# Issuing the weight-sum transfers of an output projection some steps sooner, and after the last heads' merges on GpSimd

## The chip, the cores and the metric

The kernel runs on one core of one Trainium2 chip. The metric is the time of one execution on the device in microseconds (us); lower is better. The engines are TensorE (PE; its weight loads are listed as PEld), VectorE (DVE), ScalarE (ACT), GpSimd (POOL) and SyncE (SP). Each takes its instructions in a fixed order, and a transfer (DMA) is an instruction in the order of the engine that issues it.

## The reference, cut to what matters

One layer of a transformer-like block over 512 tokens of width 1024, in fp32: a gated linear attention and a latent attention with 8 heads, merged by gates, then an output projection, then a feed-forward layer.

```python
n = rmsnorm(h, g_mix[l])
proj = n @ w_in[l]
...
y_gla = gla_branch(gq, gk, gv, gr, z_gf, z_gb, ...)
y_mla = mla_branch(cq, ckv, kr, positions, ...)          # softmax attention, 8 heads
merged = jax.nn.sigmoid(z_ma) * y_gla + jax.nn.sigmoid(z_mb) * y_mla
h = h + merged @ w_out[l]                                # 512x1024 times 1024x1024
m = rmsnorm(h, g_mlp[l])
h = h + jnp.square(jax.nn.relu(m @ w_ff1[l])) @ w_ff2[l]
...
return rmsnorm(h, g_final)
```

## The kernel before

Every matmul operand is split into a high and a low part (`split`: ACT copies to the high part, then DVE or POOL subtracts to get the low part, lines 93 and 94), and each product is three matmuls (`mm3`, lines 88 to 90).

**The attention loop.** It runs `n` from 0 to 37. Step `n` does the scores and the exponential of one head and one quarter of the tokens (`att_scores`, `s`, `e`, lines 1017 and 1022), normalises earlier ones (line 1029), transposes (`att_flip`, `tp`, `pT`, line 1037), and every second step multiplies with the values (`att_values`, `av`). When a head is finished, `merge` scales its output on DVE (`tb`, line 1065) and adds the other branch on POOL (`mx`, `my`, line 1068). Heads 2p and 2p+1 fill the two column halves of one pair of tiles, `mx` and `my` of pair p. The last head, 7, merges in two halves: `mx` when its first 256 tokens are ready, `my` with the others. `LAG_C` is 6, so the values of head 6 come at n = 31 and 33, and those of head 7 at n = 35 and 37.

**The projection** multiplies by seven products of half-size blocks instead of eight (products 1, 2, 5, 6, 3, 7, 4, in this order). Its left operands are made pair by pair: `gao` from `mx` (`split_first`, products 1 and 2; its first 256 columns belong to the pair's even head and to product 1, the others to the odd head and product 2), and the sums `yo` and `zo` (`merged_sums`, lines 938 to 941) with their splits `ghyo`, `glyo`, `ghzo`, `glzo` (`split_sum`, products 5, 6, 7, 3). For pair 3 these sums are made after the loop on DVE (`ghbo`, `glbo`, `ghco`, `glco`).

Its right operands are blocks B11, B12, B21, B22 of `w_out`, and sums of them:

- Products 1 and 2 take B11 and B21 as they are (`streamed`, tiles `bo10`, `bo11`, `bo20`, `bo21`; 11 and 13, 21 and 23 are their steps).
- The tiles `w_00`, `w_01` hold block B11, to which `load_onto(B11, B12)` adds B12 (product 5). `w_20`, `w_21` are loaded with B22, then B11 is added, then B12 (product 6), and later B21 (product 4). `w_10`, `w_11` hold B12, to which B22 is added (product 7); `w_30`, `w_31` hold B22 (product 3).
- A plain load (`load_w2`, line 903) is four 256 KB transfers issued by SP. An adding transfer (`load_onto`, line 909) is two 512 KB transfers issued by POOL with an accumulating write, and each waits until what was written to that tile before has landed:

```python
for g, d in enumerate(block_tiles(dst)):
    ...
    nc.gpsimd.dma_start(d, rows.rearrange(...)[:, x // 2], accum_op=ALU.add)
```

After the loop the code of the projection fixes the order of PE, ACT and DVE by hand (`in_program_order(begun, PE_ONLY + SPLITTERS)`), and the order of POOL from the start of the attention loop on is the order of the program text (`in_program_order(attending, (...Pool,))`). In the attention itself a list scheduler orders PE, ACT, DVE and SP. The first four column blocks of the feed-forward weights are `f00f` to `f03f` (line 223), loaded by SP into a ring of three staging buffers that `bo20f` and `bo21f` use too. `goes_behind(late, early, engines)` puts the first instruction of one group behind the last of another on an engine.

Of the kernel before, what the change touches and what calls it, by code (L numbers as in the profile page):

```python
# [56 lines left out]
def tile_block(ctx: ExitStack, tc: tile.TileContext, t, out: bass.AP):  # L57
    nc = tc.nc
# [48 lines left out]
    def traced():  # L107
        return len(nc.cur_bb.bb.instructions)

    def in_program_order(start, engines=None):  # L110

        prev = {}
        for ins in nc.cur_bb.bb.instructions[start:]:
# [4 lines left out]
                issued_after(ins, before)  # L118
            prev[ins.engine] = ins.name

    PE_ONLY = (mybir.EngineType.PE,)
    SPLITTERS = (mybir.EngineType.Activation, mybir.EngineType.DVE)

    def goes_behind(late, early, engines):

        ins = nc.cur_bb.bb.instructions
        for e in engines:
            a, b = [[i for i in ins[x:y] if i.engine == e] for x, y in (early, late)]
            if a and b:
                issued_after(b[0], a[-1].name)  # L130
# [115 lines left out]
    def proj_run(begun, src, half=None, ks=range(KD)):  # L246
        wh, wl, acc = begun
        c = slice(0, S) if half is None else slice(half * 256, half * 256 + 256)
        for k in ks:
            mm3(acc[:, c], wh[:, k, :], wl[:, k, :], src[k][:, 0, c], src[k][:, 1, c], k == 0, k == KD - 1)  # L250
        return acc
# [620 lines left out]
    def split_sum(left, src, m_lo, m_hi, name, rest=nc.vector):  # L872
        h, l = u2(f"gh{name}", F32R), u2(f"gl{name}", F32R)
        split(h, l, src, rest)
        left[m_lo] = h[:, 0:HT], l[:, 0:HT]
        left[m_hi] = h[:, HT:S], l[:, HT:S]
# [22 lines left out]
    def load_w2(qd, x, w=w2, block=None):  # L899

        for g, dst in enumerate(block_tiles(x)):
            for pp_ in range(2):
                nc.sync.dma_start(dst[:, pp_, :], block_rows(w, qd, x if block is None else block, g, pp_))

    def load_onto(dst, x, w):

        for g, d in enumerate(block_tiles(dst)):
            rows = w[4 * g * P : 4 * (g + 1) * P, (x % 2) * S : (x % 2 + 1) * S]
            nc.gpsimd.dma_start(d, rows.rearrange("(k t p) w -> p t k w", t=2, p=P)[:, x // 2], accum_op=ALU.add)  # L909
# [24 lines left out]
    def merged_sums(p, eng):  # L934
        px, qx = merged[p]
        a11, a12, a21, a22 = px[:, 0:HT], px[:, HT:S], qx[:, 0:HT], qx[:, HT:S]
        y, z = u2(f"yo{p}"), u2(f"zo{p}")
        eng.tensor_tensor(y[:, 0:HT], a21, a22, op=ALU.subtract)
        eng.tensor_tensor(y[:, HT:S], y[:, 0:HT], a11, op=ALU.subtract)
        eng.tensor_tensor(z[:, 0:HT], a11, a21, op=ALU.subtract)  # L940
        eng.tensor_tensor(z[:, HT:S], a12, y[:, HT:S], op=ALU.add)
        return y, z
# [99 lines left out]
    def att_values(head, half):  # L1042
        if half == 0:
            avs[head] = ps("mm", f"av{head}")
        acc = avs[head]
        hi, lo = pTs.pop((head, half))
        _, _, vs, c = heads[head]
        for k in range(NT):
            vt = vs[k // 2]
            mm3(acc[:, half * 256 : (half + 1) * 256], vt[:, 0, k % 2, c], vt[:, 1, k % 2, c],  # L1050
                hi[:, k, :], lo[:, k, :], k == 0, k == NT - 1)
        if head < MH - 1:
            if half == 1:
                merge(head, acc, (0, 1))
        else:
            merge(head, acc, (half,))
# [51 lines left out]
    for n, (a, m) in enumerate(steps[:-4]):  # L1108
        ahead = steps[n + 2]
        if a == 0:  # L1110
            for x in {3: (0,), 7: (2, 1), 4: (3,)}.get(m, ()):
                sevens[1].load(x)
        if steps[n + 1] in fillers:
            at = traced()
            begun[steps[n + 1]] = fillers[steps[n + 1]][0]()
            goes_behind((at, traced()), loading, (mybir.EngineType.SP,))
        if n == 1:
            split_sums(x_y, 5, 6)
        if n == 2:
            split_sums(x_z, 7, 3)  # L1120
        if (a, m) == (0, 5):
            load_gates()
            pos_i = u2("pos_i", I32)
            nc.gpsimd.dma_start(pos_i, t["positions"][0].partition_broadcast(P))
        if (a, m) == (0, 4):
            z_chunk_finish(z_acc)
            split_gates()
        if (a, m) in fillers:
            sevens[a].product(m)
            sevens[ahead[0]].prepare(ahead[1])  # L1130
            rest = fillers[a, m][1](begun.pop((a, m)))
            if (a, m) == (0, 6):
                z_acc = rest
        elif m == 7:
            sevens[a].multiply(m)
            sevens[ahead[0]].prepare(ahead[1])
            sevens[a].sinks(m)
        else:
            sevens[ahead[0]].prepare(ahead[1])
            sevens[a].product(m)  # L1140
# [114 lines left out]
    units = up_units(1)  # L1255
    next(units)
    attending = traced()
    sums_of, flipping = {}, {}
    for n in range(4 * MH + LAG_C):
        if n % 2 == 0 and 2 <= n <= 4 * MH:  # L1260
            att_normalise((n - 2) // 4, (n - 2) % 4)
        scored = traced()
        if n < 4 * MH:
            att_scores(n // 4, n % 4)
            if n - 2 in flipping:
                goes_behind((scored, traced()), flipping[n - 2], SPLITTERS)
        scored = scored, traced()
        if 2 <= n % 8 < 7:
            next(units, None)
        if n in (6, 14):  # L1270
            units = up_units(n // 8 + 2)
            next(units)
        b = n - LAG_B
        if 0 <= b < 4 * MH:
            flips = traced()
            att_flip(b // 4, b % 4)
            flipping[n] = flips, traced()
            if b == 0:
                gla_turn(GH - 1, (flips, traced()))

        extra = traced()
        for x, at in (("y", (18, 26, 32)), ("z", (20, 28, 33))):
            if n in at:
                p = at.index(n)
                to = (5, 6) if x == "y" else (7, 3)
                split_sum(wo_left[p], sums_of[p, x], *to, f"{x}o{p}", nc.gpsimd)
        if n in (19, 30):
            p = (19, 30).index(n)
            split_first(wo_left[p], merged[p][0], f"o{p}", nc.gpsimd)
        if n < 4 * MH:  # L1290
            goes_behind((extra, traced()), scored, SPLITTERS[:1])
        if n == 35:
            split_first(wo_left[2], merged[2][0], "o2")
        if n in (11, 13):
            streamed(1, B11, (n - 11) // 2)
        if n in (21, 23):
            streamed(2, B21, (n - 21) // 2)
        if n == 22:
            load_w2(0, B11, w_out)
        if n == 23:  # L1300
            load_w2(0, B21, w_out, B22)
        if n == 25:
            load_onto(B11, B12, w_out)
        if n == 27:
            load_onto(B21, B11, w_out)
        if n == 28:
            load_w2(0, B12, w_out)
            load_w2(0, B22, w_out)
        if n == 31:
            load_onto(B21, B12, w_out)  # L1310
        if n == 34:
            load_onto(B12, B22, w_out)
        c = n - LAG_C
        if c >= 0 and c % 2 == 1:
            att_values(c // 4, (c % 4) // 2)
        if c > 0 and c % 8 == 7 and c // 8 < NP - 1:
            sums_of[c // 8, "y"], sums_of[c // 8, "z"] = merged_sums(c // 8, nc.gpsimd)

    hrow = []
    for i in range(NT):  # L1320
# [12 lines left out]
    def first_half_square(i, c):  # L1333
        hparts[i] = sm(f"hp{i}", 4)
        ms_rows[i] = u4(f"ms{i}", F32, (P, D))
        square_half(hrow[i], c, hparts[i], ms_rows[i], True)

    span = {}

    def second_half_square(i, c):  # L1340
        square_half(hrow[i], c, hparts[i], ms_rows[i], False)
# [43 lines left out]
    def hidden(qd, j):  # L1385

        if qd == 0 and j < 2:
            acc = early[j][2]
        elif qd == 0 and j in (2, 3):
            at = traced()  # L1390
            begun = proj_begin(w1, j * P, f"f{qd}{j}")
            goes_behind((at, traced()), span["norm", NT - 1] if j == 2 else span["evacuate", 1], SPLITTERS)
            acc = proj_run(begun, mT)
        else:
            acc = proj_run(proj_begin(w1, (qd * FQ + j) * P, f"f{qd}{j}"), mT)
        a = u2(f"fa{qd}{j}")
        nc.scalar.activation(a, acc, AF.Relu)  # L1397
        return a
# [154 lines left out]
    fm.evacuate(0, range(4, KD))  # L1553
    first_half_square(3, 1)
    span["evacuate", 0] = at, traced()
    early = [proj_begin(w1, 0, "f00", "mm")]
    wo_product(4, (0,))
    add_rows(2, 0, xs_[0])
    second_half_square(2, 0)
    early.append(proj_begin(w1, P, "f01", "mm"))  # L1560
    wo_product(4, (1,))
    at = traced()
    add_rows(3, 0, xs_[1])
# [90 lines left out]
```

## Time and profile before

| | |
|---|---|
| median of 3 runs | 775.52 us (775.02 to 776.52) |
| the profiled execution's own time | 775.01 us |
| its span, first to last instruction | 773.3 us |
| PE, PEld busy | 757.3 us (98%), 638.1 us (83%) |
| DVE, ACT, POOL busy | 579.7 us (75%), 453.4 us (59%), 152.0 us (20%) |
| TensorE clock granted, mean | 0.997 |
| chain that ended last | PE 87%, DVE 3%, ACT 3%, POOL 2%, DMA 2%, issue 2% |

"Busy" counts the time in which at least one instruction of the engine runs; on PE the instructions overlap, so that the time between two starts (0.23 us for a 128x512 matmul, 0.12 for 128x256) says more than a duration. The attention loop lies at about 305 to 389 us, the projection at 384 to 434, and the feed-forward layer follows to the end.

### The profile page before, as it was taken

How to read it: one execution, taken by the hardware profiler on the slowest of the kernel's cores; microseconds unless marked ns; L12 is line 12 of the kernel's file. 1: busy time of each engine (PE TensorE's matmuls, PEld its weight loads, DVE VectorE, ACT ScalarE, POOL GpSimd, SP SyncE). 2: the span in 40 equal slices, each digit the busy share in tenths (PEclk: the TensorE clock that was granted, in tenths of full speed). 3: DMA queues.
4: the chain of work that ended last, by engine and by line, in shares of the span. 5: the costliest groups of instructions: out<-in, count | busy, mean ns of one | idle time of the engine just before them, and what ended most of it. 6: DMA issues, size and time to landing. Idle time of an engine off the chain costs nothing.

```text
span 773.3 us, 10231 instructions
## 1 busy us (share of the span) xinstructions
PE 757.3 (98%) x3744; PEld 638.1 (83%) x3744; DVE 579.7 (75%) x848; ACT 453.4 (59%) x768; POOL 152.0 (20%) x228
## 2 busy tenths in 40 slices
PE   9999999999999999999979999999999999999996
PEld 7888788889888889898958788888888888888885
DVE  7789999666677766999947776965787578848695
ACT  8456567565466555888825675444644465336644
POOL 0720006160623114045852000000000000000014
PEclk9999999999999999999999999999999999999999
DMA  9733201121324324114997331263115510560002
GB/s 311 248 110 119 79 27 29 55 83 45 90 58 119 51 58 126 44 48 140 282 250 194 109 109 55 68 201 112 55 36 182 158 34 28 174 181 0 28 1 109
DMA packets 97185, 81.28 MB, mean 105 GB/s; under 512 B 15504, under 2 KB 74896, under 8 KB 97136
## 3 DMA queue, kind: packets, MB, share of 16 engines
q1 hardware_dynamic: 93904, 74.33, 31.9%
q0 software_dynamic: 2944, 6.03, 4.2%
q8 instruction: 29, 0.48, 0.3%
q10 hardware_dynamic: 288, 0.28, 0.1%
q14 instruction: 20, 0.16, 0.1%
HBM read 76.96 MB, written 2.10 MB: 102 GB/s over the span
## 4 chain that ended last, share of the span: by engine, by line
PE 87%; DVE 3%; ACT 3%; POOL 2%; DMA 2%; issue 2%; POOLq 0%; SPq 0%; DVEq 0%; ACTq 0%
PE f L89 7%; PE f L90 7%; PE f L88 7%; PE gx L88 4%; PE gx L89 4%; PE gx L90 4%; PE first L326 3%; PE za L88 2%; PE za L89 2%; PE gz L88 2%; PE za L90 2%; PE gz L89 2%; PE gz L90 2%; DMA w<-in_w_out 2%; PE zb L88 1%
## 5 line engine op out<-in xcount | busy, mean ns | idle before, releaser
L1593 POOL DMA_DIRECT2D gfin<-in_g_final x1 | 0.6, 625 | 283.0 <-PE f L90 283.0
L913 DVE TENSOR_TENSOR w<-w,w 128x1024 f32<-128x1024 f32 x32 | 38.7, 1221 | 0.3
L474 POOL COPY v3f<-rrf 128x4 f32<-128x4 f32 x4 | 2.8, 709 | 135.9 <-DVE rrf L457 135.9
L1022 ACT ACTIVATE e<-s,top 128x512 f32<-128x512 f32 x32 | 21.9, 686 | 6.8 <-DVE top L1017 6.5
L1329 DVE TENSOR_TENSOR h<-h,gx 128x512 f32<-128x512 f32 x32 | 21.5, 682 | 1.9 <-PE gx L90 1.8
L94 DVE TENSOR_TENSOR pT<-tp,pT 128x512 fp32r<-128x512 f32 x32 | 21.7, 682 | 1.6 <-ACT pT L93 1.4
L1017 DVE TENSOR_REDUCE top<-s 128x1 f32<-128x512 f32 x32 | 21.6, 679 | 0.9 <-PE s L90 0.7
L1037 PE MATMUL tp<-ident,e 128*128 128x128 f32 x128 | 19.4, 275 | 0.8 <-ACT e L1028 0.8
L93 ACT ACTIVATE pT<-tp 128x512 fp32r<-128x512 f32 x32 | 18.9, 596 | 1.3 <-PE tp L1037 1.0
L88 PE MATMUL av<-pT,v 128*128 128x256 f32 x64 | 19.0, 296 | 0.0
L89 PE MATMUL av<-pT,v 128*128 128x256 f32 x64 | 18.5, 289 | 0.0
L1397 ACT ACTIVATE fa<-f 128x512 f32<-128x512 f32 x32 | 18.5, 578 | 0.0
L93 ACT ACTIVATE ghb<-y 128x512 fp32r<-128x512 f32 x16 | 10.1, 632 | 14.0 <-DVE y L859 14.0
L90 PE MATMUL av<-pT,v 128*128 128x256 f32 x64 | 18.0, 282 | 0.0
L94 DVE TENSOR_TENSOR sc<-sc,sc 128x512 fp32r<-128x512 f32 x16 | 10.9, 691 | 9.5 <-ACT sc L93 9.5
L1037 PEld LDWEIGHTS tp<-ident,e 128*128 128x128 f32 x128 | 14.9, 141 | 3.7 <-ACT e L1028 1.5
L93 ACT ACTIVATE sc<-sc 128x512 fp32r<-128x512 f32 x16 | 9.3, 596 | 11.5 <-DVE sc L545 11.5
L909 POOL DMA_DIRECT2D w<-in_w_out x10 | 12.7, 1454 | 13.5 <-DVE bo60l L94 6.7
L93 ACT ACTIVATE b_00h<-w 128x1024 fp32r<-128x1024 f32 x7 | 7.4, 1059 | 12.3 <-PE gz L90 6.0
L93 ACT ACTIVATE b_20h<-w 128x1024 fp32r<-128x1024 f32 x7 | 7.4, 1061 | 12.1 <-PE gz L90 6.0
L93 ACT ACTIVATE b_10h<-w 128x1024 fp32r<-128x1024 f32 x7 | 7.4, 1061 | 12.1 <-PE gx L90 6.0
L88 PE MATMUL s<-kbuf,q 96*128 96x512 f32 x32 | 14.3, 447 | 0.1
(1665 smaller groups left out, 2939.1 us busy)
## 6 DMA issues: line engine op xcount, KB each, us to landing
w<-in_w_ff SPq DMA_DIRECT2D x64, 256.0 KB, 3.4
w<-in_w_out POOLq DMA_DIRECT2D x10, 512.0 KB, 10.3
grw<-in_w_in SPq DMA_DIRECT2D x8, 512.0 KB, 9.3
gvw<-in_w_in SPq DMA_DIRECT2D x8, 512.0 KB, 4.6
w<-in_w_out SPq DMA_DIRECT2D x16, 256.0 KB, 5.8
x<-in_xt SPq DMA_DIRECT2D x8, 256.0 KB, 5.1
vw<-in_w_first SPq DMA_DIRECT2D x8, 256.0 KB, 5.3
h<-in_x SPq DMA_DIRECT2D x4, 512.0 KB, 16.3
```

Source lines behind the costliest of these rows:

```text
L88: nc.tensor.matmul(acc, lh, rh, start=start, stop=False, skip_group_check=onto)
L89: nc.tensor.matmul(acc, lh, rl, start=False, stop=False, skip_group_check=onto)
L90: nc.tensor.matmul(acc, ll, rh, start=False, stop=stop, skip_group_check=onto)
L93: nc.scalar.activation(hi, src, AF.Copy)
L94: rest.tensor_tensor(lo, src, raw(hi), op=ALU.subtract)
L326: nc.tensor.matmul(f_accs[i], a[:, i * P : (i + 1) * P], b, start=k == 0 and x == 0, stop=k == KD - 1 and x == 2)
L913: nc.vector.tensor_tensor(wq[dst][g], wq[x][g], wq[y][g], op=op)
L1017: nc.vector.tensor_reduce(top, acc, axis=AX.X, op=ALU.max, negate=True)
L1022: nc.scalar.activation(e, acc, AF.Exp, bias=top, accum_out=tot[:, qt % 2 : qt % 2 + 1])
L1037: nc.tensor.transpose(tp[:, k * P : (k + 1) * P], e[:, k * P : (k + 1) * P], ident)
L1329: nc.vector.tensor_tensor(hc, hc, acc, op=op)
L1397: nc.scalar.activation(a, acc, AF.Relu)
```

## The change

The adding transfers and the plain loads in front of them move to earlier steps; the second addition onto B21 moves behind the merges of head 6, and that onto B12 behind those of head 7. The low halves of the sums of pair 2 go from POOL to DVE and some steps later. Four loads of feed-forward columns get an order on SP: none goes ahead of the loads of step 17.

```diff
+    SP_ONLY = (mybir.EngineType.SP,)
...
-    sums_of, flipping = {}, {}
+    sums_of, flipping, span = {}, {}, {}
...
+        if n == 20:
+            load_onto(B11, B12, w_out)
         extra = traced()
-        for x, at in (("y", (18, 26, 32)), ("z", (20, 28, 33))):
+        for x, at in (("y", (18, 26, 34)), ("z", (20, 28, 36))):
             if n in at:
                 p = at.index(n)
                 to = (5, 6) if x == "y" else (7, 3)
-                split_sum(wo_left[p], sums_of[p, x], *to, f"{x}o{p}", nc.gpsimd)
+                split_sum(wo_left[p], sums_of[p, x], *to, f"{x}o{p}", nc.gpsimd if p < 2 else nc.vector)
...
-        if n == 22:
+        if n == 15:
             load_w2(0, B11, w_out)
+        if n == 17:
+            at = traced()
+            load_w2(0, B21, w_out, B22)
+            span["sums"] = at, traced()
         if n == 23:
-            load_w2(0, B21, w_out, B22)
-        if n == 25:
-            load_onto(B11, B12, w_out)
-        if n == 27:
             load_onto(B21, B11, w_out)
-        if n == 28:
+        if n == 24:
             load_w2(0, B12, w_out)
             load_w2(0, B22, w_out)
-        if n == 31:
-            load_onto(B21, B12, w_out)
-        if n == 34:
-            load_onto(B12, B22, w_out)
         c = n - LAG_C
         if c >= 0 and c % 2 == 1:
             att_values(c // 4, (c % 4) // 2)
+        if n == 33:
+            load_onto(B21, B12, w_out)
         if c > 0 and c % 8 == 7 and c // 8 < NP - 1:
             sums_of[c // 8, "y"], sums_of[c // 8, "z"] = merged_sums(c // 8, nc.gpsimd)
+    load_onto(B12, B22, w_out)
...
             begun = proj_begin(w1, j * P, f"f{qd}{j}")            # f02, f03
             goes_behind((at, traced()), span["norm", NT - 1] if j == 2 else span["evacuate", 1], SPLITTERS)
+            goes_behind((at, traced()), span["sums"], SP_ONLY)
...
+    at = traced()
     early = [proj_begin(w1, 0, "f00", "mm")]
+    goes_behind((at, traced()), span["sums"], SP_ONLY)
...
+    at = traced()
     early.append(proj_begin(w1, P, "f01", "mm"))
+    goes_behind((at, traced()), span["sums"], SP_ONLY)
```

In the built program this gives these orders around the change. POOL: `glyo` and `gao` of pair 0, the two adds onto `w_00`, `w_01`; `glzo` of pair 0, the merges of head 3, the sums of pair 1, the two first adds onto `w_20`, `w_21`; the merges of head 4, `glyo` and `glzo` of pair 1, the merges of head 5, the sums of pair 2, `gao` of pair 1, the merges of head 6; then the two second adds onto `w_20`, `w_21`; the merges of head 7; the two adds onto `w_10`, `w_11`. SP: the loads of `w_00`, `w_01`, `w_20`, `w_21`, then `bo21f`, `f00f`, `f01f`, `f02f`, then those of `w_10`, `w_11`, `w_30`, `w_31`. DVE: `glyo` of pair 2 ahead of its `gao`, `glzo` of pair 2 between the two scalings `tb` of head 7. The scheduler's order on PE, ACT and DVE changes by a few places between heads 4 and 7, with the same instructions.

More of the change, by code (lines that the diff above doesn't have):

```diff
@@ L1115, in tile_block @@
             begun[steps[n + 1]] = fillers[steps[n + 1]][0]()
-            goes_behind((at, traced()), loading, (mybir.EngineType.SP,))
+            goes_behind((at, traced()), loading, SP_ONLY)
         if n == 1:
@@ L1336, in first_half_square @@
         square_half(hrow[i], c, hparts[i], ms_rows[i], True)
-    span = {}
     def second_half_square(i, c):
```

## The prediction

> **What bounds the kernel now.** PE is busy for 98% of the span, so I first asked what PE waits for. The list of waits, PE alone, from 383 to 447 us:
>
> ```profile
> PE wox L88 <- ACT gao L93: 5.3, 1, 5.3
> PE f L90 <- DVE f01l L94: 0.4, 1, 0.4
> ```
>
> One wait is 5.3 us; the others are below half a microsecond. Busy time by stretches (the columns are the engines' busy time and counts, then the granted clock, the DMA share and GB/s) shows what follows it:
>
> ```profile
> 390.60:396.10 5.50, 0.17 (x1) 0.00 (x0) 0.01 (x1) 0.46 (x2) 4.88 (x6) 0.98 1.09 296
> 396.10:399.60 3.50, 3.50 (x9) 2.55 (x10) 2.09 (x2) 1.02 (x2) 3.50 (x5) 0.54 1.09 193
> 399.60:404.00 4.40, 4.40 (x21) 3.64 (x20) 3.69 (x7) 2.83 (x4) 0.53 (x1) 1.00 0.90 185
> ```
>
> PE stands still, then runs 3.5 us at a clock of 0.54, then at 1.00. The timeline of PE gives the length exactly:
>
> ```profile
> 390.39 0.39 PE L90 MATMUL wox<-bo11h,gao 128*128 128x512 f32 x1
> ...
> 396.11 0.79 PE L88 MATMUL wox<-bo11h,gao 128*128 128x512 f32 x1 [5.33 <-ACT gao L93]
> ...
> 399.57 0.40 PE L90 MATMUL wow<-bo20h,gao 128*128 128x512 f32 x1
> ```
>
> It waits for `gao` of pair 3, which ACT makes from `mx` of head 6. The timeline of DVE has that head's scaling early, and the timeline of POOL says why `mx` is late:
>
> ```profile
> 382.96 0.67 DVE L1065 SCALAR_TENSOR_TENSOR tb<-tb,av 128x512 f32<-128x512 f32 x1
> ```
>
> ```profile
> 367.88 2.54 POOL L909 DMA_DIRECT2D w<-in_w_out  x2
> ...
> 374.44 2.45 POOL L909 DMA_DIRECT2D w<-in_w_out  x2
> ...
> 383.00 1.29 POOL L94 TENSOR_TENSOR gao<-mx,gao 128x512 fp32r<-128x512 f32 x1
> 386.52 1.20 POOL L909 DMA_DIRECT2D w<-in_w_out  x1 [2.23 <-DMA w<-in_w_out]
> 391.22 1.20 POOL L909 DMA_DIRECT2D w<-in_w_out  x1 [3.50 <-DMA w<-in_w_out]
> 391.97 1.75 POOL L94 TENSOR_TENSOR glyo<-yo,ghyo 128x512 fp32r<-128x512 f32 x1
> 393.20 1.73 POOL L94 TENSOR_TENSOR glzo<-zo,ghzo 128x512 fp32r<-128x512 f32 x1
> 394.42 1.19 POOL L1068 TENSOR_TENSOR mx<-tb,za 128x256 f32<-128x256 f32 x1
> ```
>
> `tb` of head 6 is done at 383.6, but `mx` stands behind the second adds onto `w_20` and `w_21`. Each waits for the first add to its tile (issued from 374.44 on) to land, and behind them come the splits of pair 2's sums. ACT makes `gao` at 395.64, PE starts at 396.11.
>
> **What the stall costs.** PE would have started at 390.39 + 0.23 = 390.62, so it is 5.49 us late. The next eight matmuls take 399.57 - 396.11 = 3.46 us instead of 8 x 0.2275 = 1.82 (21 starts from 399.81 to 404.58), so the low clock costs 1.64 more. Together 7.13 us, if nothing else takes the place of the wait.
>
> **Merges of head 6 ahead of the second adds.** POOL's work up to `gao` of pair 1 keeps its pace: the first adds onto `w_20`, `w_21` take the place at 367.9 that those onto `w_00` had, and the merges, sums and splits behind wait for DVE and ACT as before. `gao` ends at 384.3, `mx` and `my` of head 6 (0.73 and 0.92) at 385.0 and 385.9. ACT is free for `gao` of pair 3 at about 385.4 (its last pieces in this place end at 385.5 now), done 385.8. DVE makes the low half behind `tb` of head 7's second half (388.52 + 0.42), so at about 389.4. PE needs it at 390.62: the wait goes, with 1.2 us to spare.
>
> **The two splits moved to DVE.** Two 128x512 subtractions at 0.69 us (the row of `gao` there has 693 ns) are 1.4 us more on DVE between 385 and 389. DVE now waits 1.88 us for PE ahead of the scaling at 388.52, which covers them. POOL loses 2 x 1.29 us.
>
> **Head 7's merges behind the second adds.** The first adds are issued at 367.9 and 369.1 and landed at most 15.7 us after issue (the list of transfers has this for the one issued at about 377, the slowest), so by 384.8. The second adds then start without a wait at 385.9 and 387.1, and `mx`, `my` of head 7 run from 388.3 to 389.9 (`tb` is ready at 386.6 and 388.9). ACT has `bo50h` ahead, which waits for PE's last use of `bo10` (389.4) and takes 1.04; `gao`'s second half ends at 390.9, its low half behind `bo50l` (1.22 + 0.50) at 392.1. PE needs it for the last pair of product 2, at 390.62 + (6 + 18) x 0.2275 = 396.1. Slack 4 us.
>
> **The sums of blocks.** The second adds land 10.4 us (the issue at 386.5 now) after 385.9 and 387.1: 396.3 and 397.5. ACT splits from there (1.06), DVE 1.22 later behind the additions of product 1 and 2: about 398.6 and 401. Product 6 starts at 390.62 + 54 x 0.2275 = 402.9 and wants `bo61` at 405.6. At the slowest 15.7 they land at 401.6 and 402.8, `bo60` is split at 403.9 and `bo61` at about 406: under 1 us of stall, and perhaps 1 us more through DVE, which is busy from 402.9 to 418 now. I take 0: of the 3 MB that SP issued from 365.6 to 373, ahead of these transfers, the 1 MB for `w_20`, `w_21` is gone by then, and the first adds run 6.5 us sooner. The add onto `w_10` goes out at 389.9 instead of 395.8 for a split now at 413.0.
>
> **SP and the loads moved.** Eight transfers of 256 KB (four took 1.95 us of SP) now stand ahead of `bo21f`, `f00f`, `f01f`. The last four wait for head 2's values, whose scaling begins at 347.65, so `bo21f` goes out at about 350 instead of 346.6 and lands 2.9 us later; ACT takes it at 361.5 now. `f00f` to `f02f` went out at 348.8 to 365.2 for splits at 432 to 441. Cost 0, cover 8 us or more. `w_00` and `w_20` land (5.8 us, the page's median) by 356, before POOL's adds want them.
>
> **The reordered attention.** DVE takes `bo20l` (1.21) and a few others some places earlier. Now PE is busy 40.0 of 40.0 us from 320 to 360 and its waits for `e` at 310.7 and 362.5 are 0.25 and 0.51. From below -0.8 (these go), from above +1.75 (the longest single DVE row there, `bo21l`, in full); I take 0, by the 40.0 row.
>
> **The tail of the projection** (DVE, ACT, POOL and PE in turns, 418 to 444) starts from PE's product 3 and moves with it. Nothing in it depends on an absolute time: the third adds onto `w_20` go out behind `bo60l` as now and land in 6 to 7.2 us for a split 15 us later.
>
> **Sum.** 775.01 - 7.13 = 767.9 for an execution like the profiled one, which lies 0.5 under the median: 768.4.
>
> **The rivals.**
> *A part of the wait comes back* (`bo60` late by the slowest landing, or PE waits in the attention): against it speak the slacks above, for it that DVE has no idle time in the projection. The slowest landing costs 2, the attention 1.75: up to 772.1. A short stall keeps the clock: the idle times of 0.5 us left it at 1.00. The Trainium skill (TensorE: Matmul & The Clock Gate, "HAM oscillation") puts the limit at an idle time of about 3.4 us; the trace has nothing between 0.5 and 5.5. By that rule a new stall of 4 us costs 4 + 1.64: 774.0.
>
> *The change doesn't do what it says*: another instruction on POOL, ACT or DVE holds `gao` back as long as before, 775.5. The order of the built program speaks against it.
>
> *Slower: POOL blocks at the second adds with head 7's merges behind.* They are still in one queue, and now `my` of head 7 and all sums of pair 3 come after them. PE is where it was before when `gao`'s second low half comes 5.5 us after 396.1, at 401.6; `mx` 1.7 us earlier (0.73 + 0.42 + 0.50), the issue of `w_21` (1.20) before it: a first add that lands at 398.7, 29.6 us after its issue. Beyond, each us costs one: 34 us would give 780. For it speaks that POOL waited 2.23 and 3.50 us at this place and that the DMA share was over 1; against it, 15.7 us as the slowest of all.
>
> **How the numbers follow.** 0.2% (1.55 us) is about what a measurement of this kernel can tell from no change. The full gain 0.74, with its own range 767.3 to 770.2 (-0.8 and +1.75 of the attention, some 0.3 of spread); a part of it 0.13, 770 to 774; no change 0.05; slower 0.08, by the blocked queue or an attention that loses over 8 us. Faster by over 0.2% is 0.74 + 0.13 = 0.87. The range leaves out the slower and unchanged cases and the upper third of the partial one: 766.8 to 772.5.
>
> **What would show it.** PE's wait of 5.33 at `wox` gone, its clock 1.00 from 385 to 430; `mx` of head 6 at about 384.3 ahead of L909; no DMA wait on POOL there; product 2 at about 392.0, the first `mb` at 416.5 instead of 423.6. It is wrong if PE waits over 1 us at `wow` or product 6, or if the first `wox` of the projection starts later than 383.6 by over 1 us.

## The result and the profile after

The changed kernel takes 768.11 us (median of 4 runs, 768.01 to 768.70) where the kernel before takes 776.02 (775.02 to 776.63): a ratio of 0.9901 with a 95% interval of 0.9884 to 0.9918. In a second comparison it is 768.36 against 776.37 us, 0.9897 [0.9884, 0.9910]. The profiled executions are 768.70 us (span 767.0) and 767.94 us (span 766.2).

The list of PE's waits from 383 to 447 us in the profile after (total, times, longest) has three lines:

```profile
PE f L90 <- DVE f01l L94: 0.4, 1, 0.4
PE wox L88 <- DVE h L1331: 0.3, 1, 0.3
PE f L89 <- DVE mT L98: 0.3, 1, 0.3
```

The wait of 5.3 us for `gao` is gone and no other has come in this stretch. The three stretches that stood at a clock of 0.98, 0.54 and 1.00 before (columns as there):

```profile
390.60:396.10 5.50, 5.50 (x26) 4.56 (x25) 4.32 (x9) 2.99 (x5) 3.00 (x3) 1.00 1.12 203
396.10:399.60 3.50, 3.50 (x17) 2.92 (x16) 3.50 (x6) 1.85 (x3) 0.26 (x1) 1.00 1.05 225
399.60:404.00 4.40, 4.40 (x21) 3.62 (x21) 4.01 (x6) 2.74 (x7) 3.02 (x4) 1.00 1.10 259
```

PE is busy through all of them at 1.00. The timeline of GpSimd shows the new order (start, length):

```profile
383.85 1.28 POOL L94 TENSOR_TENSOR gao<-mx,gao 128x512 fp32r<-128x512 f32 x1
385.09 0.73 POOL L1069 TENSOR_TENSOR mx<-tb,za 128x256 f32<-128x256 f32 x1
385.79 0.73 POOL L1069 TENSOR_TENSOR my<-tb,za 128x256 f32<-128x256 f32 x1
386.48 2.41 POOL L910 DMA_DIRECT2D w<-in_w_out  x2
388.10 1.55 POOL L1069 TENSOR_TENSOR mx<-tb,za 128x256 f32<-128x256 f32 x1
390.36 0.86 POOL L1069 TENSOR_TENSOR my<-tb,za 128x256 f32<-128x256 f32 x1 [0.71 <-DVE tb L1066]
```

`mx` and `my` of head 6 follow `gao` of pair 1 at once, and the two second adds (L910) start without a wait for a transfer. On VectorE the moved splits are the first and the third line here:

```profile
386.20 0.88 DVE L94 TENSOR_TENSOR glyo<-yo,ghyo 128x512 fp32r<-128x512 f32 x1
387.00 0.68 DVE L94 TENSOR_TENSOR gao<-mx,gao 128x512 fp32r<-128x512 f32 x1
...
387.93 0.68 DVE L94 TENSOR_TENSOR glzo<-zo,ghzo 128x512 fp32r<-128x512 f32 x1
389.86 0.42 DVE L1066 SCALAR_TENSOR_TENSOR tb<-tb,av 128x256 f32<-128x256 f32 x1 [1.25 <-PE av L90]
```

VectorE still waits 1.25 us for PE behind them (1.88 before), so they are covered. Where PE stands is read from its timeline:

```profile
384.60 0.39 PE L88 MATMUL wox<-bo10h,gao 128*128 128x512 f32 x1
...
392.86 0.39 PE L88 MATMUL wow<-bo20h,gao 128*128 128x512 f32 x1
...
417.35 1.04 PE L199 MATMUL mb<-ident,ms 128*128 128x128 f32 x8
```

These three marks and the first `uq` after 286 us (the up-projection of queries, just ahead of the attention) cut every profile of this study into four pieces. The place of that `uq` lies between 291.8 and 293.0 us from run to run, with equal code ahead of it; the pieces behind it repeat within 0.15 us for equal kernels, so parts are weighed by them:

| us | uq to wox (attention) | wox to wow | wow to mb | mb to the end | sum |
|---|---|---|---|---|---|
| before, both profiles | 90.89, 90.91 | 15.30, 15.45 | 24.72, 24.65 | 349.68, 349.63 | 480.6 |
| after, both profiles | 92.00, 92.01 | 8.26, 8.30 | 24.49, 24.49 | 349.65, 349.57 | 474.4 |
| difference | +1.10 | -7.10 | -0.20 | 0 | -6.2 |

The stall gave back 7.1 us, and the attention took 1.1 of it.

### The profile page after: what moved, and what is told of

Its sections match the earlier page's. It is cut to its first block, busy times and chain, and to the rows that moved or that the text cites. A ratio compares the mean times of both kernels' runs of the same rounds, so it can differ in the third digit from the quotient of the medians.

```text
span 767.0 us, 10229 instructions
## 1 busy us (share of the span) xinstructions
PE 755.7 (99%) x3744; PEld 637.4 (83%) x3744; DVE 579.7 (76%) x850; ACT 453.5 (59%) x768; POOL 149.6 (20%) x226
## 4 chain that ended last, share of the span: by engine, by line
PE 91%; DVE 4%; ACT 3%; issue 1%; POOL 0%; DMA 0%; POOLq 0%; SPq 0%; ACTq 0%; DVEq 0%
PE f L89 7%; PE f L90 7%; PE f L88 7%; PE gx L88 4%; PE gx L90 4%; PE gx L89 4%; PE first L327 3%; PE za L88 2%; PE za L89 2%; PE gz L88 2%; PE za L90 2%; PE gz L89 2%; PE gz L90 2%; PE zb L88 1%; PE zb L90 1%; PE zb L89 1%
## 5 line engine op out<-in xcount | busy, mean ns | idle before, releaser
L88 PE MATMUL av<-pT,v 128*128 128x256 f32 x64 | 19.1, 298 | 0.4 <-ACT pT L93 0.4
L88 PE MATMUL s<-kbuf,q 96*128 96x512 f32 x32 | 14.3, 446 | 0.4 <-DVE pT L94 0.4
L1407 ACT ACTIVATE px<-fa 128x256 f32<-128x256 f32 x32 | 13.4, 418 | 1.0
```

Source lines behind the costliest of these rows:

```text
L88: nc.tensor.matmul(acc, lh, rh, start=start, stop=False, skip_group_check=onto)
```

## The experiments

The edit has three parts: the **order** on GpSimd (second adds and the adds onto `w_10` behind the merges), the **transfers** (loads and first adds some steps sooner, with the order on SP), and the **splits** of pair 2's sums on VectorE. Each was run alone, and each was left out.

**The order alone.** The kernel before, with

```diff
-        if n == 31:
-            load_onto(B21, B12, w_out)
-        if n == 34:
-            load_onto(B12, B22, w_out)
...
+        if n == 33:
+            load_onto(B21, B12, w_out)
...
+    load_onto(B12, B22, w_out)
```

> The kernel before with one part of the change: the second adds onto B21 behind the merges of head 6, the add onto B12 behind those of head 7. Loads and first adds stay at their old steps, the low halves of pair 2 stay on POOL. Theory A (what stands ahead of the merges on POOL): gao of pair 1 ends at 384.3, two splits of 1.3 follow, mx of head 6 ends at 387.6, gao of pair 3 at about 388.2, before PE needs it at 390.6: the wait of 5.3 us and the low clock go. The second adds now start at 388.5 and 391.2 (the first ones land no sooner), so bo60 and bo61 are some 2.5 us later than in the changed kernel and PE may wait up to 2 us there: 768.5 to 771. Theory B (the gain comes from the transfers being spread out earlier): the wait stays, 774.5 or more. Theory C (the gain comes from the two splits leaving POOL): 775.

769.88 us, 0.9914 [0.9901, 0.9928]. The stall is gone and the time is in the range of theory A: wox to wow is 9.19 us, of which PE waits 0.6 for `tb`. But mb to the end has grown from 349.6 to 351.44 us. The splits and the merges go first here, and the second adds still wait for first adds issued late; the timeline of GpSimd, and that of ACT where the sum is used:

```profile
388.29 1.20 POOL L910 DMA_DIRECT2D w<-in_w_out  x1
392.12 1.21 POOL L910 DMA_DIRECT2D w<-in_w_out  x1 [2.64 <-DMA w<-in_w_out]
```

```profile
401.46 1.06 ACT L93 ACTIVATE bo61h<-w 128x1024 fp32r<-128x1024 f32 x1 [2.61 <-DMA w<-in_w_out]
```

ACT takes `bo61h` 8.98 us behind the first `wow`, against 5.64 in the changed kernel. VectorE is then busy but for 0.87 us from `bo61l` (402.56) to 413.5, and PE waits for its `h`:

```profile
PE wox L88 <- DVE h L1331: 2.1, 2, 1.8
```

**The transfers alone.** The kernel before, with

```diff
-        if n == 22:
+        if n == 15:
             load_w2(0, B11, w_out)
-        if n == 23:
+        if n == 17:
             load_w2(0, B21, w_out, B22)
...
-        if n == 25:
+        if n == 20:
             load_onto(B11, B12, w_out)
-        if n == 27:
+        if n == 23:
             load_onto(B21, B11, w_out)
-        if n == 28:
+        if n == 24:
             load_w2(0, B12, w_out)
             load_w2(0, B22, w_out)
```

and the order of `f00f` to `f03f` on SP behind them.

> The kernel before with the loads and the first adds at the earlier steps, and nothing else: the second adds still stand ahead of the merges of head 6, then the splits of pair 2 on POOL. Theory A: the first adds have landed by 382, so the second adds start at 385.1 without a wait and take 2.4, the two splits 2.6, mx 0.7: mx ends at 390.8, gao at 391.3, PE waits 1 us at most and keeps its clock: 768.5 to 769.5, since what cost time was the wait for the landing, and that goes here too. Theory B: the full gain, 768. A strict reading of the order (any add ahead of the merges costs): 771 or more. Theory C: 775.

774.35 us, 0.9970 [0.9959, 0.9982]: only the theory of a strict order is not contradicted, and its mechanism is another. No second add waits for a transfer. GpSimd runs through in one piece, and VectorE stands still beside it; the timelines of GpSimd and of VectorE:

```profile
386.74 2.22 POOL L94 TENSOR_TENSOR glyo<-yo,ghyo 128x512 fp32r<-128x512 f32 x1
387.98 2.18 POOL L94 TENSOR_TENSOR glzo<-zo,ghzo 128x512 fp32r<-128x512 f32 x1
389.20 1.63 POOL L1069 TENSOR_TENSOR mx<-tb,za 128x256 f32<-128x256 f32 x1
389.88 2.08 POOL L1069 TENSOR_TENSOR my<-tb,za 128x256 f32<-128x256 f32 x1
```

```profile
386.76 4.64 DVE L94 TENSOR_TENSOR gao<-mx,gao 128x512 fp32r<-128x512 f32 x1 [0.30 <-ACT gao L93]
391.32 0.41 DVE L1066 SCALAR_TENSOR_TENSOR tb<-tb,av 128x256 f32<-128x256 f32 x1
```

A subtraction that takes 0.68 us in the changed kernel takes 4.64 here, from just behind the start of `glyo` (386.74) to 391.40, while the last of the four, `my`, runs to 391.96. `tb` of head 7 stands behind it, and PE waits 3.80 us for `tb` (`PE av L88`). The clock between 390.6 and 396.1 is 0.70, so the half clock is back too: wox to wow is 13.84 us, 5.56 more than in the changed kernel.

**The splits alone.** The kernel before, with

```diff
-        for x, at in (("y", (18, 26, 32)), ("z", (20, 28, 33))):
+        for x, at in (("y", (18, 26, 34)), ("z", (20, 28, 36))):
...
-                split_sum(wo_left[p], sums_of[p, x], *to, f"{x}o{p}", nc.gpsimd)
+                split_sum(wo_left[p], sums_of[p, x], *to, f"{x}o{p}", nc.gpsimd if p < 2 else nc.vector)
```

> The kernel before with the low halves of pair 2 moved to DVE, and nothing else: mx of head 6 follows the second add onto w_21 directly. Theory A: mx starts at about 392.0 instead of 394.4, PE starts 2.4 us sooner, after an idle time of 3.0 us. 773.1 if the low clock of 3.4 us follows an idle time of 3 us too, 771.5 if it doesn't. Theory C: 768. Theory B: 775.

773.15 us, 0.9957 [0.9943, 0.9970], the time that theory A gives with a low clock, though the wait is 3.6 us and not 3.0. The second adds wait 2.71 and 3.75 us ahead of `mx` of head 6, PE waits 3.6 us at `wox` for `gao`, and the low clock still follows (0.53 from 393.6 to 397.0).

**The change with one part left out.** Each of the three diffs is undone in the changed kernel. The changed kernel ran once more beside the runs without the splits and without the order, and came out as expected; the run without the early transfers belongs to the comparison of the parts alone, so its median is set beside the others only through the kernel before and through the pieces.

> The changed kernel itself, once more, as the yardstick for the three others on the same chip: 767.5 to 769 us, 0.988 to 0.992 of the kernel before.

> The changed kernel with the loads and the first adds back at the old steps: merges of head 6 ahead of the second adds, low halves of pair 2 on DVE. Theory A: mx of head 6 ends at 385.0, the second adds start at 386.5 and 391.2, as before, and merges of head 7 follow at 392.4, in time for PE's 396.1. bo61 comes about 2 us later than in the changed kernel: PE waits 0 to 1.5 us at product 6. 767.5 to 769.5. The attention keeps the order of the kernel before, in which PE reached the projection 0.9 us sooner than in the changed one. Theory B: 774.

> The change without its third part: the low halves of pair 2's two sums are split on GpSimd again, after gao of pair 1 and ahead of head 6's merges. The adds stay behind the merges and early. GpSimd then works without a gap on two-input operations from 383.9 to about 389.3 (gao, glyo, glzo, mx, my). Theory A (only GpSimd's queue counts, as the prediction reckoned): mx is 2.6 us later, at 387.7, ACT's gao of pair 3 at 388.8, DVE's low half by 390.0, all ahead of PE's need at 391.6: the time of the changed kernel within 0.5 us. Theory B (a two-input operation of VectorE is held off while GpSimd runs such operations back to back, as in the run of the early transfers alone, where one took 4.64 us in place of 0.69): a DVE row between 385 and 391 is stretched to 2 us or more, PE waits over 1 us for what stands behind it, and the time is 1.5 to 5 us above the changed kernel's.

> The change without its order on GpSimd: the transfers and first adds are early and the two splits are on VectorE, but the second adds onto w_20, w_21 and the adds onto w_10 stand ahead of the merges of head 6 and of head 7 again. The second adds start without a wait at 385.1 and take 2.4 us, so mx of head 6 is at about 387.7, ACT's gao at 388.8, PE's need at 391.6. Theory A (the order is worth something only while the first adds land late or the splits are in the queue): the time of the changed kernel within 0.7 us, no wait of PE over 0.5 us from 384 to 400. Theory B (the order is the part that carries the gain): PE waits over 1 us at wox and the time is 1 to 5 us above the changed kernel's.

| us | median | ratio to before | PE's largest wait, 384 to 430 | uq to wox | wox to wow | mb to the end |
|---|---|---|---|---|---|---|
| all three | 768.36 | 0.9897 [0.9884, 0.9910] | 0.3 | 92.01 | 8.30 | 349.57 |
| no early transfers | 769.45 | 0.9909 [0.9895, 0.9922] | 1.8 `h` | 90.91 | 8.41 | 351.73 |
| no splits on VectorE | 769.39 | 0.9909 [0.9896, 0.9922] | 0.5 `tb` | 92.01 | 9.01 | 349.55 |
| no order | 770.30 | 0.9922 [0.9910, 0.9935] | 1.6 `tb` | 92.05 | 10.10 | 349.65 |
| the order alone | 769.88 | 0.9914 [0.9901, 0.9928] | 1.8 `h` | 90.90 | 9.19 | 351.44 |

Three things follow. By the pieces, the early transfers buy the tail (351.7 to 349.6 us, 2.1) and sell the attention (90.9 to 92.0, 1.1): about 1 us net. The ratios say the same size, but their intervals overlap. Without them the time lies at the top of theory A's range, and PE's wait stands at `h` in the tail, not at product 6. With the transfers early, the order is not what removes the wait for the first adds: without it the second adds start with no wait too (the timeline of GpSimd):

```profile
384.94 2.43 POOL L910 DMA_DIRECT2D w<-in_w_out  x2
```

What it removes then is a hold of VectorE, 1.6 us of PE's time: theory A of that run fails (770.30 against 768.36), theory B has the size and the wrong place: PE waits at `av`, for `tb`, and not at `wox`. The hold in that run, on VectorE:

```profile
387.04 2.34 DVE L94 TENSOR_TENSOR gao<-mx,gao 128x512 fp32r<-128x512 f32 x1
```

And without the splits on VectorE the same subtraction takes 1.55 us beside `glzo` and costs PE 0.5: theory A is missed by 0.5 us of the medians (by 0.2 in the sum of the pieces, 475.06 against 474.4), and theory B holds in kind, with a shorter row and wait than it gives and 0.5 us under its lowest time. The intervals of this run and the changed kernel overlap, so here too the pieces carry the reading.

**What holds VectorE off.** The changed kernel with 5 us of work on GpSimd that nobody uses, between `my` of head 6 and the second adds: once additions, which read SBUF (`lock_read`), and once memsets, which only write (`lock_write`).

```diff
         if n == 33:
+            extra = traced()
+            idle = u2("idle")
+            for _ in range(4):                      # lock_read
+                nc.gpsimd.tensor_tensor(idle, merged[2][0], merged[2][0], op=ALU.add)
+            for _ in range(10):                     # lock_write, in place of the four
+                nc.gpsimd.memset(idle, 0.0)
+            begin = traced()
             load_onto(B21, B12, w_out)
+            goes_behind((begin, traced()), (extra, begin), (mybir.EngineType.Pool,))
```

> The changed kernel with extra work on GpSimd that nobody uses: four additions of a 128x512 tile in SBUF to itself (1.25 us each by the rows of gao, 5.0 us in all) behind my of head 6 and ahead of the second adds. The order on the other engines is the changed kernel's. Theory A (a VectorE operation with two SBUF inputs is held off by a GpSimd queue that reads SBUF, as long as that queue runs back to back): one of glyo, gao, glzo on VectorE, which take 0.7 to 0.9 us, is stretched to 4 us or more, tb of head 7 behind it is late, PE waits 2.5 to 4 us for it at av, a half clock of 3.4 us follows, and the time is 771.5 to 774.5. Theory B (the stretched rows of the earlier runs had another cause, the transfers or what VectorE itself waits for): VectorE's rows stay at 0.7 to 0.9 us; only the second adds are 5 us later, and the time is 768.5 to 770.

> As lock_read, but the 5 us of extra work on GpSimd are ten memsets of a 128x512 tile (0.54 us each in the profile of the kernel before), which read nothing from SBUF. Theory A (the hold is by GpSimd's reads): VectorE's glyo, gao, glzo stay at 0.7 to 0.9 us, no wait of PE over 1 us for tb; the second adds start 5 us later, at about 390.8, and gao's second half comes at about 396, where PE needs it: 768.5 to 770. Theory A' (any work of GpSimd holds VectorE off): the same as lock_read, 771.5 to 774.5. By the prediction's slack of 4 us at head 7's merges, 5 us of delay there should cost PE about 1 us.

771.10 us (0.9933 [0.9918, 0.9948]) and 771.11 (0.9931 [0.9914, 0.9947]). The times are equal and the traces are not. VectorE's `gao` and `glzo` rows, which have two inputs, first beside the four additions (GpSimd 386.86 to 392.36):

```profile
387.37 1.52 DVE L94 TENSOR_TENSOR gao<-mx,gao 128x512 fp32r<-128x512 f32 x1
...
389.15 1.19 DVE L94 TENSOR_TENSOR glzo<-zo,ghzo 128x512 fp32r<-128x512 f32 x1
...
391.42 1.22 DVE L94 TENSOR_TENSOR gao<-mx,gao 128x256 fp32r<-128x256 f32 x1
```

and then beside the ten memsets (386.69 to 392.48):

```profile
387.24 0.68 DVE L94 TENSOR_TENSOR gao<-mx,gao 128x512 fp32r<-128x512 f32 x1
...
388.17 0.68 DVE L94 TENSOR_TENSOR glzo<-zo,ghzo 128x512 fp32r<-128x512 f32 x1
...
390.44 0.42 DVE L94 TENSOR_TENSOR gao<-mx,gao 128x256 fp32r<-128x256 f32 x1
```

Beside the additions the three rows are 0.84, 0.51 and 0.80 us longer than beside the memsets: what holds these two-input operations of VectorE off here is that GpSimd reads SBUF. (`glyo`, which starts 0.3 us ahead of the first addition, takes 0.88 us in both runs.) The Trainium skill (SBUF — State Buffer, "Who interferes with whom") states that kind: VectorE with two inputs in SBUF contends with a GpSimd instruction that reads SBUF, not with one that only writes. The Trainium skill (SBUF — State Buffer, "Summary: rules for kernel authors") says that of such a pair the second one to issue blocks until the first finishes. By that rule the wait for one instruction is at most as long as that instruction, as in these three rows (an addition took 1.38 us); the 4.64 us beside four instructions is longer.

So the kind of the hold is shown, and why it lasted over nearly the whole row of four there is not. In the two runs with the long rows (4.64 and 2.34 us) GpSimd's operations stood right behind transfers that it issued, in the three with shorter ones (1.74 in the order alone, 1.55 and 1.52) they did not; that is an observation on five rows. GpSimd's own rows overlap there (the two adds of the transfers alone reach from 385.23 to 387.65, `glyo` starts at 386.74), so which of its instructions held VectorE at what time can't be read from them.

Theory A's size for `lock_read` (a row of 4 us, a wait of 2.5 to 4, a half clock) is a miss; PE waits 0.6. The time of `lock_write` is 1.1 us above its range, though its rows are as theory A has them and not as A' has. Both times come from elsewhere: the second adds are some 5.6 us later against `wox`, ACT takes `bo61h` of the run with memsets 9.73 us behind `wow`, PE waits 1.8 for `h` as in the order alone, and mb to the end is 351.5 and 351.8 us.

**Only the first adds changed places.** The changed kernel without the early transfers, with

```diff
         if n == 25:
-            load_onto(B11, B12, w_out)
+            load_onto(B21, B11, w_out)
         if n == 27:
-            load_onto(B21, B11, w_out)
+            load_onto(B11, B12, w_out)
```

> A version of the change with the transfers from HBM left at their old steps: the order on GpSimd and the splits on VectorE as in the change, and of the first adds only the two pairs change places, those onto w_20, w_21 at step 25 and those onto w_00, w_01 at step 27. Theory A (what the early transfers bring is only that the first adds onto w_20 have landed when the second ones come up, and what they cost is the attention's order, about 1 us): second adds without a DMA wait, or one under 0.7 us, no wait of PE over 1 us at h, and a time of 767 to 768.5, at or under the changed kernel's. Theory B (loads that early are needed): a DMA wait of over 1.5 us on GpSimd at the second adds and 768.5 to 770. The instructions of the attention get yet another order on PE, worth between 0 and 1 us either way, which no theory here forecasts.

771.86 us (769.81 to 772.59), 0.9936 [0.9922, 0.9949]; neither theory. In the profiled execution the second adds do not wait, but the first ones do:

```profile
370.74 1.30 POOL L910 DMA_DIRECT2D w<-in_w_out  x1 [3.51 <-PE tp L1038]
372.92 1.22 POOL L910 DMA_DIRECT2D w<-in_w_out  x1 [0.89 <-DMA w<-in_w_out]
```

The second of these rows names the transfer that it waits for, the load of its tile. The first is put down to PE's `tp`, which was done by 370.15; the loads of `w_20`, `w_21` went out from 364.9 on, so it was probably a load as well. Everything behind them on GpSimd is later (`gao` of pair 1 at 385.42, while PE started `wox` at 383.53), VectorE is held off twice (rows of 1.28 and 1.22 us) and PE waits 1.0 for `tb`. So to change the places of the adds alone does not do what the early transfers do. The trace is that of the fastest execution (769.81 us, mean clock 0.999). Four of the six took 771.7 to 772.6 at 0.996 to 0.997, and where they lost the other 2 us no trace shows.

**The attention's old order, pinned.** The changed kernel, with PE's, ACT's and VectorE's instructions from the attention to the end of the first projection chained in the order of the kernel without the early transfers. GpSimd and SP keep the changed order.

```diff
+    PINNED = {
+        mybir.EngineType.PE: (
+            (0, 77), (91, 92), (77, 84), (92, 103), (132, 133), (84, 87), (117, 118), (133, 135), (118, 124),
...
+    for e, pieces in PINNED.items():
+        mine = [i for i in nc.cur_bb.bb.instructions[attending:early_at] if i.engine == e]
+        rank = [k for a, b in pieces for k in range(a, b)]
+        for x, y in zip(rank, rank[1:]):
+            issued_after(mine[y], mine[x].name)
```

> The changed kernel with the attention's old order: on PE, ACT and VectorE the instructions from the attention to the end of the first projection are chained in the order that they have in the kernel without the early transfers; GpSimd and SP keep the changed kernel's order. Theory A (the 1.10 us by which the attention is longer in every run with the early transfers, 92.0 us against 90.9 from the first uq after 291 to the first wox, come from the order of its instructions, not from the transfers): 90.9 us again, no DMA wait over 0.5 us at the second adds, 766.8 to 767.6. Theory B (the transfers themselves or VectorE and ACT waiting for the later bo21f lengthen it): 91.5 to 92.5 us and 768 to 769.

767.80 us (767.60 to 768.09), 0.9890 [0.9875, 0.9904], where the changed kernel had 0.9897 and 0.9901; 0.2 above theory A's range. uq to wox is 90.74 us, as theory A has it, wox to wow 8.50, mb to the end 349.66, the sum 473.4 instead of 474.4. Up to 395 us the traces of this run and of the kernel without the early transfers show the same order of instructions on the three engines. The attention's 1.1 us are thus the price of the order that the scheduler made on those engines, not of the transfers. The sum of the pieces says 1.0 us, the medians 0.3 to 0.6; as the intervals overlap, only the pieces show this version ahead of the changed kernel.

**The kernel before, a second profile.**

> The kernel before once more, for a second profiled execution. The times of the kernel before spread over 2.5 us (775.0 to 777.6), those of the changed one over 1.1. Theory A (its stall passes on how late the first adds land, and the first profile had a short one): the DMA waits on GpSimd at the second adds sum to another figure than 5.73 us, and first wox to first wow is longer or shorter than 15.30 us by as much. Theory B (the spread lies elsewhere, ahead of the attention or in the tail): 15.30 us within 0.2 and the first uq, at 292.71, elsewhere by 0.5 or more.

774.57 us. The second adds wait 2.66 + 3.23 = 5.89 us (5.73 in the first) and wox to wow is 15.45 us: the stretch is longer by as much as the waits (0.15 and 0.16), as theory A has it, but that is far from the 2.5 us of spread; theory B has the stretch right and misses at `uq`, which moved by 0.45 (292.26 against 292.71) and not by 0.5 or more. Both profiled executions of the kernel before lie at the low end of its times (775.0 to 777.6 in these comparisons), so neither shows a long one. The medians differ by 7.9 to 8.0 us and the profiles by 6.3 to 6.6; where the other 1.5 or so lie is open, since only profiled executions leave a trace. The mean granted clock, which every execution has, narrows it: 0.997 in both profiled executions of the kernel before, 0.991 to 0.995 in the 28 others where it is known (0.991 in all six above 777 us), and 0.997 to 0.999 in the eight of the changed kernel. So the kernel before ran at a lower mean clock when it was not profiled; a mean does not say at which place, and whether this is all of the 1.5 us was not tried.

## Why the prediction was right

768.4 us was forecast, 768.11 and 768.36 came. Step by step:

- **The stall and its low clock, 7.13 us.** Measured 7.1 (15.30 and 15.45 to 8.26 and 8.30). Runs with one part of the change show the same two terms: a wait of 3.80 us costs 5.56, the low clock being the other 1.76, and one of 3.64 costs 5.32.
- **Merges of head 6.** `mx` was to start at 384.3; it did at 385.09 in a run that was 1.0 late at `wox`, and at 384.34 in the other. ACT's `gao` came 1.4 and 0.6 us later than reckoned, as the high halves `ghyo` and `ghzo` go ahead of it; the low half on VectorE, forecast to be ready at about 389.4, was ready at 390.6 and 389.9.
- **Splits on VectorE.** 0.88 and 0.68 us, reckoned at 0.69 each, covered as said. What the step did not see is what they are worth on the other side: on GpSimd they hold VectorE off. That costs 0.7 us of wox to wow with the rest of the change (9.01 against 8.30), and 3.7 where only the transfers are early (13.84, against 10.10 in the run without the order, which has the transfers and the splits).
- **Head 7's merges behind the second adds.** No wait for a transfer, second low half forecast for 392.1, there at 392.3 in the second profile. With the second adds 5.7 us later (memsets) PE still did not wait at `wow` (8.29 us), so the slack was more than the 4 us given.
- **The sums of blocks, taken at 0.** Right, and it is the early transfers that make it so: without them, or with the second adds delayed, `bo61h` is 3.3 to 4.1 us later against `wow` and the tail takes 1.8 to 2.2 us more. The prediction had put "under 1" and "perhaps 1" on that case.
- **The loads on SP, taken at 0.** Right: pinned has the same order on SP and the attention of before.
- **The reordered attention, taken at 0 with -0.8 and +1.75 as bounds.** This is the mis-sized term: +1.1 (1.08 to 1.16) in all seven profiles with the early transfers and the scheduler's own order, gone when the old order is chained. The row "PE busy 40.0 of 40.0 us" from 320 to 360 did not bear on it: the new waits lie behind 360. The list of PE's waits from 300 to 384 in the second profile after has

```profile
PE s L88 <- DVE pT L94: 0.4, 1, 0.4
PE av L89 <- DVE pT L94: 0.4, 1, 0.4
PE av L88 <- ACT pT L93: 0.4, 1, 0.4
PE tp L1038 <- ACT e L1029: 0.2, 1, 0.2
```

  1.4 us where the kernel before had 0.8 for `e`. The other 0.5 of the 1.1 stands in no wait of that list.
- **The step to the median, +0.5.** The kernel before lies further above its profiled executions (1.0 to 2.0 us) than the prediction's three runs showed; the changed kernel's medians lie 0.6 below the first of its own and 0.4 above the second. With +1.1 for the attention and -0.2 for wow to mb, the sum for a profiled execution is 768.8; the two had 768.70 and 767.94. That the forecast met the median within 0.3 us is in part luck: the attention's +1.1 and the missing +0.5 offset each other, and the start of the attention alone moves by up to 1.2 us from run to run.

The signs that the prediction named came: the clock is 1.00 from 385 to 430 us, product 2 starts at 392.86 and 392.14 (forecast 392.0), the first `mb` at 417.35 and 416.63 (416.5). One sign of being wrong was close: the first `wox` is 1.00 us later than 383.6 in the first profile, where "over 1 us" was the limit, and 0.24 in the second.

Of the rivals, "a part of the wait comes back" happened in the attention, at 1.1 us and without the low clock. "Slower by the blocked queue" did not: the second adds waited for no transfer.

## What to carry to other kernels

When a late instruction stands in a queue behind others, moving it ahead can bring most of the gain (here 6.7 of 8 us by the order alone); the companions of such a move are worth pricing one by one, because each can be there for a wait that the others would open. An engine's queue is not only its own: check which two-input operations of VectorE run beside SBUF reads of GpSimd, for a delay there showed up as a longer row and not as a wait of VectorE. And when a moved transfer makes a scheduler reorder a stage that it does not touch, look at the waits of that whole stage, or pin the old order.

## What the runs showed of the hardware

- A two-input VectorE operation of 0.68 us took 1.19 to 4.64 beside operations of GpSimd that read SBUF, and 0.68 beside its memsets.
- PE's clock stayed at 1.00 after waits of 0.6, 1.0, 1.6 and 1.8 us and fell to half after waits of 3.6, 3.8, 5.3 and 5.5, each time at a price of about 1.7 us (1.64 to 1.76). The limit of some 3.4 us that the Trainium skill gives (TensorE: Matmul & The Clock Gate, "HAM oscillation") lies between these; nothing here narrows it further.
- The adding transfers landed sooner in the changed kernel, in a median of 8.0 us against 10.3 in the kernel before; why was not tried. With the second adds some 5.6 us later (`lock_read`, `lock_write`) it is 10.4. The lists of transfers of the kernel without the early transfers, and of the changed kernel (second profile), end the line with the median from issue to landing:

```profile
w<-in_w_out POOLq DMA_DIRECT2D x10, 512.0 KB, 11.2
```

```profile
w<-in_w_out POOLq DMA_DIRECT2D x10, 512.0 KB, 8.0
```
